# Up projection as seven half-sized products over two pairs of PSUM tiles, with its weight sums made in DRAM

## The chip, the cores and the metric

The kernel runs on one core of one Trainium2 chip. The metric is the device time of one execution in microseconds; lower is better.

## The reference

One layer of a decoder trunk over 512 tokens of width 1024, in float32. Three attention branches (differential, stick-breaking, dilated windows) are read from one input projection, gated and merged, and pass an output projection; then a LayerNorm, and the part that the change touches:

```python
D_MODEL = 1024
SEQ = 512
D_FF = 4 * D_MODEL
PLE_DIM = 256
...
x <- LayerNorm(alpha * x + mixer(x))
x <- LayerNorm(alpha * x + MLP(x) + sigmoid(x W_g) * (p[i] W_p))
```

`MLP(x)` is `square(relu(x @ w_up)) @ w_down`, with `w_up` of 1024 x 4096 and `w_down` of 4096 x 1024.

## The kernel before

Every float32 product is made of three matmuls on rounded operands: each operand is split into a high part (ScalarE casts it, L206 for weights) and a low part (VectorE subtracts, L208), and high x high, high x low and low x high are added in PSUM. Weights come in *chunks* of 128x1024 (512 KB): `fill` issues their loads on SP into a ring of 7 raw tiles, `split_next` turns a raw tile into `wh` and `wl`, which have rings of 7 as well. So a load runs up to 14 chunks ahead of its use.

The work is a list of *items*. Each has a matmul part `mm`, an evacuation `ev` and the chunks that are free after it. The main loop at the end of `trunk` goes through the list with index `n`: it makes sure that the item's chunks are split, emits the previous item's `ev`, splits up to two chunks (`pump`), advances the attention generators by one `step`, emits `mm` and splits again. The tile framework assigns tiles, makes all waits, and places an instruction whose operands are ready ahead of one that still waits, on TensorE too. PSUM has 8 banks: 2 for `mm_bank` and 6 for `at_bank`.

Items 0 to 106 are the input projection and the branches with the attention placed among them; `wout_at` is the index after them. Then come `ple_items`, `wout_items`, `pleg_items` (the gate product, from `x1T`) and `mlp_items`. The first norm runs per 128 tokens in `ln1_gen` during the output projection: VectorE, a power operation on POOL (L440), four transposes per half on TensorE (L515), then the split into `x1hT` and `x1lT` (L518, L519).

The MLP of before: `up(f)` makes 128 hidden columns for all 512 tokens, 8 k x 3 matmuls of 512 columns (L88 to L90, `mm3`), and ScalarE applies Relu and Square. The down projection of the first 7 of 8 blocks is already in seven products instead of eight (a block of 512 hidden columns, 2x2 blocks, sums of operands): `left_first` and `left_rest` make the hidden side's sums, `down` runs a product for 128 tokens (L698 to L700, columns 512). The sums of its weights are made in DRAM by DMAs from POOL: `sum_steps` yields 8 copies and accumulating copies for each block, 56 in all, one for each item from `n` = 30 on; each waits for the latest VectorE split (`st["low"]`). The last block goes through `plain`, with the second norm behind it.

Of the kernel before, what the change touches and what calls it, by code (L numbers as in the profile page):

```python
# [10 lines left out]
F32 = mybir.dt.float32  # L11
# [7 lines left out]
P = 128  # L19
# [37 lines left out]
def trunk(tc, a, out):  # L57
    nc = tc.nc
    es = ExitStack()
    with es:  # L60
# [84 lines left out]
        loads, chunks, placed = [], [], []  # L145
        st = {"dma": 0, "split": 0}
# [47 lines left out]
        def split_next():  # L194
# [9 lines left out]
            for h, lo, a0, a1 in parts:  # L204
                raw = c["from"]["raw"][:, a0:a1]
                i = nc.scalar.copy(h, raw)  # L206
                st["cast"] = getattr(i, "ins", i)
                i = nc.vector.tensor_sub(lo, raw, h.bitcast(F32))  # L208
                st["low"] = getattr(i, "ins", i)
            c["from"]["uses"] -= 1  # L210
# [265 lines left out]
        ln1_done = {}  # L476

# [22 lines left out]
        def ln1_gen(tt):  # L500
# [11 lines left out]
            for h in range(2):  # L512
# [4 lines left out]
                t3 = tp.rearrange("p (k t) -> p k t", k=4)  # L517
                nc.scalar.copy(o, t3)  # L518
                nc.vector.tensor_sub(x1Tl["b"][:, 4 * h:4 * h + 4, q], t3, o.bitcast(F32))  # L519
            ln1_done[tt] = True  # L520
            yield
# [23 lines left out]
        def pleg_items():  # L545
            for half in range(2):
                cs = [chunk(a["wg"][half, c].rearrange("p k n -> p (k n)"), 1024) for c in range(4)]
                for tt in range(4):
# [9 lines left out]
                    def ev(ps, tt=tt, half=half):  # L558
# [6 lines left out]
                        if half and tt > 1:  # L565
                            nc.vector.tensor_sub(acc[tt - 2, 1], acc[tt - 2, 1], t)
# [9 lines left out]
        wsum = [[dram.tile([P, 1024], F32, name=f"wsum{b}_{i}") for i in range(4)] for b in range(7)]  # L576

        def sum_steps():
            def steps(b):
                w = [a["wd"][b, i].rearrange("p k n -> p (k n)") for i in range(4)]  # L580
                t = wsum[b]
                yield t[0], w[0], False
                yield t[2], w[1], False
                yield t[0], w[1], True
                yield t[2], w[3], True
                yield t[1], t[0], False
                yield t[1], w[3], True
                yield t[3], t[1], False
                yield t[3], w[2], True

            def issue(o, i, plus):
# [5 lines left out]
                tc.add_manual_dep(getattr(i, "ins", i), st["low"].name, mybir.DependencyInfo(  # L597
                    mybir.DependencyClass.Sync, mybir.DependencyReason.DATA), reason="spread over the main stream")

            todo = deque(steps(b) for b in range(7))  # L600
# [12 lines left out]
        hraw = {}  # L613
        later = deque()
        left = {}
        keep = {}
        p1s = {}
        v3 = {}
        HB = slice(0, 256)
        HC = slice(256, 512)  # L620

        def mlp_items():
            nb = 7

            def up(f, free=True):
                c = chunk(a["wu"][f].rearrange("p k m -> p (k m)"), 1024)

                def mm(ps):
                    for k in range(8):
                        s = slice(k * P, k * P + P)  # L630
                        mm3(ps, c["h"][:, s], c["l"][:, s], x1T[k], x1Tl[k], k == 0, k == 7)

                def ev(ps):
                    t = slot("hid")
                    nc.scalar.activation(t, ps, AF.Relu)
                    nc.scalar.activation(t, t, AF.Square)
                    left_rest()
                    if f >= 4 * nb:
                        left[f] = split(t)
                        return  # L640
                    hraw[f] = t
                    if f % 2:
                        left_first(f // 2)
                item([c] if free else [], mm, ev)
                return c

            def split(t, cols=slice(0, 512)):
                h = slot("hh", F32R)
                lo = slot("hl", F32R)
                nc.scalar.copy(h[:, cols], t[:, cols])  # L650
                nc.vector.tensor_sub(lo[:, cols], t[:, cols], h[:, cols].bitcast(F32))
                return h, lo

            def left_first(pr):
                e, o = hraw[2 * pr], hraw[2 * pr + 1]
                s12 = slot("s12")
                nc.vector.tensor_sub(s12[:, HB], e[:, HC], o[:, HC])
                nc.vector.tensor_sub(s12[:, HC], e[:, HB], s12[:, HB])
                w = slot("hh", F32R)
                nc.scalar.copy(w[:, HB], e[:, HB])  # L660
                nc.vector.tensor_sub(w[:, HC], e[:, HB], w[:, HB].bitcast(F32))
                left[pr, 1] = (w[:, HB], w[:, HC])
                h, lo = split(s12)
                left[pr, 5] = (h[:, HB], lo[:, HB])
                left[pr, 6] = (h[:, HC], lo[:, HC])
                later.append((pr, s12))

            def left_rest():
                if not later:
                    return  # L670
                pr, s12 = later.popleft()
                e, o = hraw.pop(2 * pr), hraw.pop(2 * pr + 1)
                s34 = slot("s34")
                nc.vector.tensor_sub(s34[:, HB], e[:, HC], e[:, HB])
                nc.vector.tensor_sub(s34[:, HC], o[:, HB], s12[:, HC])
                for t, (p1, p2) in ((s34, (7, 3)), (o, (2, 4))):
                    h, lo = split(t)
                    left[pr, p1] = (h[:, HB], lo[:, HB])
# [824 lines left out]
```

## Time and profile before

| | |
|---|---|
| median of 3 runs | 1081.74 us (1081.31 to 1081.93) |
| profiled execution | 1082.02 us, its span 1080.1 us |
| granted TensorE clock | 0.998 |
| busy | PE 1069.5, PEld 893.5, DVE 661.1, ACT 478.5, POOL 70.0 us |
| up projection in the trace | from 743 to 1039 us, with the down projection among it |
| DMA | 146.18 MB, mean 135 GB/s |

PE is TensorE's matmul, PEld its weight load (beside the matmuls), DVE is VectorE, ACT is ScalarE; a q behind a name is an engine's queue of DMA issues. A line such as "L88 PE MATMUL mm<-x1hT,wh 128*128 128x512 f32 x256 | 99.6, 389 | 0.0" reads: source line, engine, operation, output from inputs, weights and moving shape, count, busy us in all, mean ns of one, idle time before. In an answer in order of time the first two numbers are start and duration in us. A line of the stretches has, after its start and end and its length, for each engine the busy us and the number of instructions (PE, PEld, DVE, ACT, POOL), then the clock, the share of the DMA engines and GB/s.

### The profile page before, as it was taken

The page shows a single profiled execution, that of the slowest core. Times are in us where ns is not written, and L with a number is a line of the kernel's source. Part 1 is how long each engine was busy: PE and PEld are TensorE (multiplying, and loading weights), DVE is VectorE, ACT ScalarE, POOL GpSimd, SP SyncE. Part 2 cuts the span into 40 slices and gives each one's busy share as a digit, 9 for nine tenths or more (in the row PEclk, how much of TensorE's full clock was granted, in tenths as well). Part 3 has the DMA queues.
Part 4 walks back from the last instruction along what each step waited for, and adds up shares of the span by engine and source line. Part 5 has one row for each costly group of instructions (what it writes and reads, how often), then busy time and mean ns, then how long its engine had stood idle before and what let it go on. Part 6 is the DMA issues. An engine that isn't in the chain of part 4 may idle for free.

```text
span 1080.1 us, 13246 instructions
## 1 busy us (share of the span) xinstructions
PE 1069.5 (99%) x4986; PEld 893.5 (83%) x4986; DVE 661.1 (61%) x1223; ACT 478.5 (44%) x795; POOL 70.0 (6%) x111
## 2 busy tenths in 40 slices
PE   9999999999999999999999999999999999999997
PEld 6888788999888888888888888888888888888886
DVE  6888667547254757655443464864575575575676
ACT  6665545425232545464233332233555454454441
POOL 0000200000111011111110020110000000000000
PEclk9999999999999999999999999999999999999999
DMA  8332313153675354567873262242244343444302
GB/s 311 129 117 90 118 40 98 51 183 98 144 208 154 119 127 166 141 162 198 244 193 111 102 231 81 89 166 98 98 158 135 137 156 136 138 146 142 122 1 78
DMA packets 43520, 146.18 MB, mean 135 GB/s; under 512 B 5593, under 2 KB 6505, under 8 KB 43457
## 3 DMA queue, kind: packets, MB, share of 16 engines
q1 hardware_dynamic: 32448, 107.93, 29.4%
q0 software_dynamic: 10432, 36.50, 13.5%
q8 instruction: 39, 0.64, 0.2%
q10 hardware_dynamic: 576, 0.92, 0.2%
q14 instruction: 25, 0.20, 0.1%
HBM read 143.21 MB, written 31.48 MB: 162 GB/s over the span
## 4 chain that ended last, share of the span: by engine, by line
PE 96%; DVE 2%; DMA 1%; ACT 0%; issue 0%; SPq 0%; DVEq 0%
PE mm L88 18%; PE mm L89 18%; PE mm L90 18%; PE mm L317 3%; PE mm L319 3%; PE mm L318 3%; PE mm L698 2%; PE mm L699 2%; PE mm L700 2%; PE at L698 2%; PE at L699 2%; PE at L700 2%; PE mm L556 1%; PE mm L490 1%; PE mm L488 1%; PE mm L554 1%
## 5 line engine op out<-in xcount | busy, mean ns | idle before, releaser
L206 ACT CAST wh<-raw 128x1024 fp32r<-128x1024 f32 (+1 forms) x201 | 207.8, 1035 | 347.1 <-PE mm L89 274.5
L208 DVE TENSOR_TENSOR wl<-raw,wh 128x1024 fp32r<-128x1024 f32 (+1 forms) x201 | 241.0, 1201 | 181.4 <-ACT wh L206 176.9
L88 PE MATMUL mm<-xhT,wh 128*128 128x512 f32 x496 | 196.3, 396 | 0.0
L89 PE MATMUL mm<-xlT,wh 128*128 128x512 f32 x496 | 194.0, 391 | 0.0
L90 PE MATMUL mm<-xhT,wl 128*128 128x512 f32 x496 | 194.0, 391 | 0.0
L90 PEld LDWEIGHTS mm<-xhT,wl 128*128 128x128 f32 x496 | 93.2, 188 | 19.5
L88 PEld LDWEIGHTS mm<-xhT,wh 128*128 128x128 f32 x496 | 93.3, 188 | 18.4 <-issue 0.2
L89 PEld LDWEIGHTS mm<-xlT,wh 128*128 128x128 f32 x496 | 93.2, 188 | 18.2 <-issue 0.2
L88 PE MATMUL mm<-x1hT,wh 128*128 128x512 f32 x256 | 99.6, 389 | 0.0
L89 PE MATMUL mm<-x1lT,wh 128*128 128x512 f32 x256 | 99.6, 389 | 0.0
L90 PE MATMUL mm<-x1hT,wl 128*128 128x512 f32 x256 | 99.6, 389 | 0.0
L317 PE MATMUL mm<-wh,xhT 128*128 128x512 f32 x160 | 64.6, 404 | 0.0
L319 PE MATMUL mm<-wh,xlT 128*128 128x512 f32 x160 | 63.1, 395 | 0.0
L318 PE MATMUL mm<-wl,xhT 128*128 128x512 f32 x160 | 62.9, 393 | 0.0
L90 PEld LDWEIGHTS mm<-x1hT,wl 128*128 128x128 f32 x256 | 48.1, 188 | 10.0
L88 PEld LDWEIGHTS mm<-x1hT,wh 128*128 128x128 f32 x256 | 48.1, 188 | 10.0
L89 PEld LDWEIGHTS mm<-x1lT,wh 128*128 128x128 f32 x256 | 48.1, 188 | 9.9
L319 PEld LDWEIGHTS mm<-wh,xlT 128*128 128x128 f32 x160 | 37.9, 237 | 3.9
L318 PEld LDWEIGHTS mm<-wl,xhT 128*128 128x128 f32 x160 | 38.1, 238 | 3.5
L317 PEld LDWEIGHTS mm<-wh,xhT 128*128 128x128 f32 x160 | 37.9, 237 | 3.5
L698 PE MATMUL mm<-wh,hh 128*128 128x512 f32 x100 | 38.9, 389 | 0.0
L699 PE MATMUL mm<-wl,hh 128*128 128x512 f32 x100 | 38.9, 389 | 0.0
(353 smaller groups left out, 1899.3 us busy)
## 6 DMA issues: line engine op xcount, KB each, us to landing
raw<-in_wt_dram SPq DMA_DIRECT2D x62, 512.0 KB, 3.6
wsum<-in_wd_dram POOLq DMA_DIRECT2D x42, 512.0 KB, 7.3
raw<-in_wu_dram SPq DMA_DIRECT2D x32, 512.0 KB, 3.3
raw<-wsum SPq DMA_DIRECT2D x28, 512.0 KB, 3.3
raw<-in_wd_dram SPq DMA_DIRECT2D x25, 512.0 KB, 3.3
raw<-in_wv_dram SPq DMA_DIRECT2D x20, 512.0 KB, 4.3
wsum<-wsum POOLq DMA_DIRECT2D x14, 512.0 KB, 4.8
raw<-in_wb_dram SPq DMA_DIRECT2D x8, 512.0 KB, 4.1
```

What stands on the lines that cost most here:

```text
L88: nc.tensor.matmul(ps, wh, xh, start=start, stop=False, skip_group_check=True)
L89: nc.tensor.matmul(ps, wh, xl, start=False, stop=False, skip_group_check=True)
L90: nc.tensor.matmul(ps, wl, xh, start=False, stop=stop, skip_group_check=True)
L206: i = nc.scalar.copy(h, raw)
L208: i = nc.vector.tensor_sub(lo, raw, h.bitcast(F32))
L317: nc.tensor.matmul(ps, x1, c["h"][:, s], start=k == 0, stop=False)
L318: nc.tensor.matmul(ps, x1, c["l"][:, s], start=False, stop=False)
L319: nc.tensor.matmul(ps, x2, c["h"][:, s], start=False, stop=k == 7)
L488: nc.tensor.matmul(ps, h[:, q], c["h"][:, s], start=k == 0, stop=False)
L698: nc.tensor.matmul(ps, h[:, q], c["h"][:, s], start=go, stop=False, skip_group_check=True)
L699: nc.tensor.matmul(ps, h[:, q], c["l"][:, s], start=False, stop=False, skip_group_check=True)
L700: nc.tensor.matmul(ps, lo[:, q], c["h"][:, s], start=False, stop=end, skip_group_check=True)
```

## The change

The up projection is made like the down projection: 8 blocks of 512 hidden columns, each as 2x2 blocks (halves of the 1024 inputs, halves of the 512 columns) against 2x2 blocks of `x1` (halves of inputs, halves of tokens), in seven products of a quarter of the work each. Each block is two column tiles (`pair(0)`, `pair(1)`) of four items: `part_a` products 2 and 1 (24 matmuls of 256 columns), `part_b` 7 and 6, `part_c` 5 (12 matmuls), `part_e` 3 and 4; the items of both pairs alternate. A pair uses one `mm_bank` (`x`) and one `at_bank` (`y`) and copies partial results to SBUF in between. A block takes 7 chunks: 3 of `w_up` itself and 4 sums from DRAM.

The sums of `x1` are made from float32 copies that `ln1_gen` now takes of its transposes (`raws`), by `x_forms` during the gate product; `last_form` writes over a quarter of `x1T` when that product is done. The down projection gets its items from `down_parts`, two blocks at a time in five stages that interleave up and down items; `left_step` makes the hidden side's operands one at a time. All products of a block are added to `acc` directly or by a chain that stays in one bank; `plain` takes the leftover products 2 and 4 of two blocks.

The DRAM sums are now 120 (8 x 8 for the up weights, 7 x 8 for the down weights), four blocks at a time, issued 1 or 2 for an item from `n` = 24 to `wout_at` − 15, none until `wout_at` + 4, and then one for every third item; each waits for the fourth last split (`lows`), not the last. The constants of the second norm are loaded at the last stage.

```diff
+                lows.append(st["low"])
             c["from"]["uses"] -= 1
...
                 t3 = tp.rearrange("p (k t) -> p k t", k=4)
+                for kp in range(2):
+                    if tt % 2 == 0:
+                        raws[h, tt // 2, kp] = slot("x1r")
+                    r3 = raws[h, tt // 2, kp].rearrange("p (k t) -> p k t", k=2)
+                    nc.scalar.copy(r3[:, :, tt % 2 * P:tt % 2 * P + P], t3[:, 2 * kp:2 * kp + 2, :])
                 nc.scalar.copy(o, t3)
                 nc.vector.tensor_sub(x1Tl["b"][:, 4 * h:4 * h + 4, q], t3, o.bitcast(F32))
...
-                            nc.vector.tensor_sub(acc[tt - 2, 1], acc[tt - 2, 1], t)
                     item(cs if tt == 3 else [], mm, ev, need=cs)
...
+            def up_steps(m):
+                w = [a["wu"][m, i].rearrange("p k n -> p (k n)") for i in range(4)]
+                a1, a2, a3, a4 = usum[m]
+                yield a1, w[2], False
+                yield a3, w[0], False
+                yield a1, w[3], True
+                yield a3, w[2], True
+                yield a2, a1, False
+                yield a2, w[0], True
+                yield a4, a2, False
+                yield a4, w[1], True
...
+            for m in range(ND):
+                todo.append(up_steps(m))
+                if m < ND - 1:
+                    todo.append(down_steps(m))
             run = []
             while todo or run:
-                while todo and len(run) < 3:
+                while todo and len(run) < 4:
                     run.append(todo.popleft())
...
+        def x_forms():
+            while len(ln1_done) < 4:
+                yield
+            r11, r12, r21, r22 = [[raws[h, th, kp] for kp in range(2)] for h in range(2) for th in range(2)]
+            for kp in range(2):
+                nc.vector.tensor_sub(r11[kp], r11[kp], r12[kp])
+                nc.vector.tensor_sub(r12[kp], r22[kp], r12[kp])
+            yield
+            fs = [split(r12[kp], "t3") for kp in range(2)]
+            forms[7] = [[fs[k // 2][i].rearrange("p (k t) -> p k t", k=2)[:, k % 2, :] for i in range(2)] for k in range(4)]
+            yield
+            for kp in range(2):
+                nc.vector.scalar_tensor_tensor(r22[kp], r22[kp], -1.0, r11[kp], op0=OP.mult, op1=OP.subtract)
+                nc.vector.scalar_tensor_tensor(r21[kp], r22[kp], -1.0, r21[kp], op0=OP.mult, op1=OP.subtract)
+            yield
+            for p, r in ((6, r22), (4, r21)):
+                gs = [split(r[kp], f"t{p}") for kp in range(2)]
+                forms[p] = [[gs[k // 2][i].rearrange("p (k t) -> p k t", k=2)[:, k % 2, :] for i in range(2)]
+                            for k in range(4)]
+                yield
...
+        def last_form():
+            for kp in range(2):
+                r = raws[0, 0, kp].rearrange("p (k t) -> p k t", k=2)
+                h, lo = [x["b"][:, 2 * kp:2 * kp + 2, HC] for x in (x1T, x1Tl)]
+                nc.scalar.copy(h, r)
+                nc.vector.tensor_sub(lo, r, h.bitcast(F32))
+            forms[5] = [(x1T[k][:, HC], x1Tl[k][:, HC]) for k in range(4)]
+            forms[1] = [(x1T[k][:, HB], x1Tl[k][:, HB]) for k in range(4)]
+            forms[2] = [(x1T[k][:, HB], x1Tl[k][:, HB]) for k in range(4, 8)]
+            forms[3] = [(x1T[k][:, HC], x1Tl[k][:, HC]) for k in range(4, 8)]
...
+            wu = a["wu"][m]
+            def operand(n):
+                src = usum[m][n] if isinstance(n, int) else wu[{"11": 0, "12": 1, "21": 2, "22": 3}[n]].rearrange(
+                    "p k n -> p (k n)")
+                cs[n] = chunk(src, 1024)
+            def pair(j):
+                js = slice(256 * j, 256 * j + 256)
+                b = {}
+                def prod(ps, p, n, start, stop):
+                    c = cs[n]
+                    for k in range(4):
+                        s = slice(512 * j + k * P, 512 * j + k * P + P)
+                        mm3(ps, c["h"][:, s], c["l"][:, s], *forms[p][k], start and k == 0, stop and k == 3)
+                def bank(n, new):
+                    def f():
+                        b[n] = new()
+                        return b[n]
+                    return f
+                def add(need, mm, ev, bank):
+                    if j == 0:
+                        for n in need:
+                            operand(n)
+                    item([cs[n] for n in need] if j else [], mm, ev, need=[cs[n] for n in need], bank=bank)
+                def part_a():
+                    def mm(ps):
+                        if 1 not in forms:
+                            last_form()
+                        prod(ps[:, HC], 2, "12", True, True)
+                        b["s"] = slot("up")
+                        nc.scalar.copy(b["s"][:, HB], ps[:, HC])
+                        prod(ps[:, HB], 1, "11", True, False)
+                    def ev(ps):
+                        if j == 0:
+                            hid[m] = [slot("hid") for _ in range(4)]
+                        nc.vector.tensor_add(hid[m][0][:, js], ps[:, HB], b["s"][:, HB])
+                    add(("12", "11"), mm, ev, bank("x", mm_bank))
+                def part_b():
+                    def mm(ps):
+                        prod(ps[:, HB], 7, 2, True, False)
+                        prod(b["x"][:, HB], 6, 1, False, False)
+                    def ev(ps):
+                        nc.scalar.copy(b["s"][:, HC], b["x"][:, HB])
+                        nc.scalar.copy(b["s"][:, HB], ps[:, HB])
+                    add((2, 1), mm, ev, bank("y", at_bank))
+                def part_c():
+                    def mm(ps):
+                        prod(ps[:, HB], 5, 0, False, False)
+                    def ev(ps):
+                        nc.vector.tensor_add(hid[m][3][:, js], ps[:, HB], b["s"][:, HB])
+                    add((0,), mm, ev, lambda: b["x"])
+                def part_e():
+                    def mm(ps):
+                        prod(b["x"][:, HB], 3, 3, False, True)
+                        prod(ps[:, HB], 4, "22", False, True)
+                    def ev(ps):
+                        nc.vector.tensor_add(hid[m][1][:, js], ps[:, HB], b["s"][:, HC])
+                        nc.scalar.activation(hid[m][2][:, js], b["x"][:, HB], AF.Relu)
+                        if j:
+                            for n, sign in ((0, 1.0), (2, 0.0), (1, -1.0), (3, -1.0)):
+                                if sign:
+                                    nc.scalar.activation(hid[m][n], hid[m][n], AF.Relu, scale=sign)
+                                nc.scalar.activation(hid[m][n], hid[m][n], AF.Square)
+                    add((3, "22"), mm, ev, lambda: b["y"])
+                return [part_a, part_b, part_c, part_e]
+            return [x for y in zip(pair(0), pair(1)) for x in y]
...
+        def left_step(m, p):
+            h = hid[m]
+            if m == ND - 1:
+                left[m, p // 2, p % 2] = split(h[p], "h")
+                return
+            if p == 7:
+                h.append(slot("l5"))
+                nc.vector.tensor_sub(h[4], h[3], h[2])
+                nc.vector.tensor_sub(h[2], h[0], h[2])
+            elif p == 6:
+                nc.vector.scalar_tensor_tensor(h[0], h[4], -1.0, h[0], op0=OP.mult, op1=OP.subtract)
+            elif p == 3:
+                nc.vector.scalar_tensor_tensor(h[0], h[1], -1.0, h[0], op0=OP.mult, op1=OP.subtract)
+            left[m, p] = split(h[{1: 0, 7: 2, 6: 0, 4: 3, 5: 4, 2: 1, 3: 0}[p]], "h")
...
+        CHAIN = {1: ("x", True, False, (0, 0), 1), 6: ("x", False, False, (2, 0), 1), 5: ("x", False, False, (2, 1), -1),
+                 3: ("x", False, True, (0, 1), -1), 7: ("y", True, False, (2, 1), -1), 4: ("y", False, True, (2, 0), 1),
+                 2: ("z", True, True, (0, 0), 1)}
+        preps = deque()
...
+        def down_parts(ms, order, kept, both=False):
+            cs = {}
+            out = []
+            for p in order:
+                for r in range(2):
+                    def part(p=p, r=r):
+                        if r == 0:
+                            cs[p] = [down_chunk(m, p) for m in ms]
+                        name, first, last, to, sign = CHAIN[p]
+                        def bank():
+                            if first:
+                                kept[name, r] = at_bank()
+                            return kept[name, r]
+                        def mm(ps):
+                            for n, m in enumerate(ms):
+                                down_mm(ps, m, p, r, cs[p][n], first and n == 0, last and n == len(ms) - 1)
+                        def ev(ps):
+                            t = acc[to[0] + r, to[1]]
+                            if sign > 0:
+                                nc.vector.tensor_add(t, t, ps)
+                            else:
+                                nc.vector.tensor_sub(t, t, ps)
+                            for _ in range(len(ms) if r == 0 or both else 0):
+                                if preps:
+                                    left_step(*preps.popleft())
+                        item(cs[p] if r else [], mm, ev, need=cs[p], bank=bank)
+                    out.append(part)
...
+            order = (1, 7, 6, 4, 5, 2, 3)
+            short = (1, 7, 6, 5, 3)
+            ups = [[0], [1, 2], [3, 4], [5, 6], [7]]
+            downs = [[], [0], [1, 2], [3, 4], [5, 6], []]
+            kept = {}
+            for stage in range(5):
+                us = [x for m in ups[stage] for x in up_parts(m)]
+                ds = down_parts(downs[stage], short if stage == 4 else order, kept, stage == 4) if downs[stage] else []
+                if stage == 4:
+                    ln2_at[0] = len(items)
+                done, lead = 0, 3
+                for n, u in enumerate(us):
+                    u()
+                    if n == len(us) - 1:
+                        nxt = downs[stage + 1]
+                        todo = [(m, p) for p in (short + (2, 4) if stage == 3 else order) for m in nxt]
+                        if stage == 4:
+                            todo = [(ND - 1, i) for i in range(4)]
+                        items[-1]["then"] = (todo, len(nxt))
+                    while done < len(ds) and (n == len(us) - 1 or done * (len(us) - lead) < (n - lead + 1) * len(ds)):
+                        ds[done]()
+                        done += 1
+            wd = a["wd"][ND - 1]
+            c2 = [down_chunk(m, 2) for m in (5, 6)]
+            cs = {(i % 2, i // 2): chunk(wd[2 * (i % 2) + i // 2].rearrange("p k n -> p (k n)"), 1024)
+                  for i in range(4)}
+            c4 = [down_chunk(m, 4) for m in (5, 6)]
+            plain(cs, c2, c4, kept)
...
             if prev is not None:
                 prev[0]["ev"](prev[1])
+                todo, lead = prev[0].get("then", ((), 0))
+                preps.extend(todo)
+                for _ in range(lead):
+                    left_step(*preps.popleft())
...
-            if n >= 30:
+            for _ in range((1 + (n % 4 == 0)) if 24 <= n < wout_at - 14 else (n % 3 == 0) if n > wout_at + 4 else 0):
                 next(sum_steps_, None)
...
-            if n == wout_at + 24:
+            if n == ln2_at[0]:
                 ln_consts("ln2_g", "ln2_b")
...
-        "wu": col_tiles(w_up[0]),
+        "wu": c(w_up[0].reshape(2, 4, 128, 8, 2, 2, 128).transpose(3, 5, 0, 2, 4, 1, 6).reshape(8, 4, 128, 2, 512)),
```

More of the change, by code (lines that the diff above doesn't have):

```diff
@@ new lines, in trunk, with split @@
+        raws = {}
+        forms = {}
+        hid = {}
+        left = {}
+        def split(t, name):
+            h, lo = slot(name + "h", F32R), slot(name + "l", F32R)
+            nc.scalar.copy(h, t)
+            nc.vector.tensor_sub(lo, t, h.bitcast(F32))
+            return h, lo
+        def x_forms():
[18 more added lines that the diff above has]
+                yield
```

324 lines of the change are left out of this document (105 added, 219 removed).

## The prediction

> **What bounds the kernel now.** I read the busy shares first, then the chain that ended last, then the waits of TensorE, then the groups of instructions by shape, and last the order of time where the change sits.
>
> ```profile
> span 1080.1 us, 13246 instructions
> ...
> PE 1069.5 (99%) x4986; PEld 893.5 (83%) x4986; DVE 661.1 (61%) x1223; ACT 478.5 (44%) x795; POOL 70.0 (6%) x111
> ...
> PE 96%; DVE 2%; DMA 1%; ACT 0%; issue 0%; SPq 0%; DVEq 0%
> ...
> PE at L298 <- ACT wh L206: 1.3, 1, 1.3
> PE at L857 <- DVE zero L854: 1.3, 1, 1.3
> PE at L1143 <- DVE lg L1138: 0.2, 1, 0.2
> ```
>
> TensorE is busy 99% of the span, the chain is 96% matmul, and between the start and the tail TensorE waits once, for 0.2 us. Time can be won only by giving it less to do, and every wait put into its stream costs in full. The 0.39 us of a "busy" matmul holds its drain; the price of one in a stream is the distance between starts:
>
> ```profile
> 799.96 0.39 PE L90 MATMUL mm<-x1hT,wl 128*128 128x512 f32 x1
> 800.19 0.39 PE L698 MATMUL mm<-wh,hh 128*128 128x512 f32 x1
> 802.91 0.39 PE L698 MATMUL at<-wh,hh 128*128 128x512 f32 x1
> ...
> 1069.24 0.39 PE L753 MATMUL at<-wh,hl 128*128 128x512 f32 x1
> 1069.47 0.28 PE L751 MATMUL at<-wh,hh 128*128 128x256 f32 x1
> 1069.67 0.69 DVE L772 TENSOR_TENSOR xn<-xn,at 128x512 f32<-128x512 f32 x1 [0.47 <-PE at L753]
> 1071.38 0.28 PE L752 MATMUL at<-wl,hh 128*128 128x256 f32 x1
> ```
>
> From 800.19 to 802.91 lie 12 starts of 512 columns: 0.2267 us each. From 1069.47 to 1071.38 lie 16 starts of 256 columns: 0.1194 us each, each with a weight load of its own. Half the columns cost 52.7% of the time, not 50%.
>
> **Term 1, the up projection: −13.6 us.** Before, 32 column tiles x 8 k x 3 matmuls are 768 of 512 columns (L88, L89, L90 on `x1hT`, 256 each): 768 x 0.2267 = 174.1 us.
>
> ```profile
> L88 PE MATMUL mm<-x1hT,wh 128*128 128x512 f32 x256 | 99.6, 389 | 0.0
> L89 PE MATMUL mm<-x1lT,wh 128*128 128x512 f32 x256 | 99.6, 389 | 0.0
> L90 PE MATMUL mm<-x1hT,wl 128*128 128x512 f32 x256 | 99.6, 389 | 0.0
> ```
>
> After, 8 blocks x 7 products x 2 column tiles x 4 k x 3 are 1344 of 256 columns: 160.5 us. A seventh product less in eight is worth 21.8 us; the shorter matmul takes 8.2 of them back. At 0.1295 us per start nothing would be left. The down projection keeps its count (7 blocks x 7 products x 12, and a plain last block), as do the tail and all before the first norm.
>
> The Trainium skill ("TensorE: Matmul & The Clock Gate", section "Back-to-back issue gap") gives N/2.4 + 2.5 ns, that is 215.8 and 109.2 ns; by it, an estimate, the term would be 165.8 − 146.7 = 19.1 us. The trace doesn't agree (226.7 and 119.4 ns), and the rows decide.
>
> **Term 2, a copy between two products in one bank: +3.2 us (0 to 9.9).** `part_a` puts product 2 into columns 256 to 511 of a PSUM bank, copies it out on ScalarE, and then puts product 1 into columns 0 to 255 of the same bank. The tile framework orders the users of a bank as a whole. The attention shows that shape: L1157 writes 128 columns of one bank for a query block, L1161 reads them, the next L1157 writes the neighbouring columns, and no reading overlaps the next writing.
>
> ```profile
> 392.77 0.60 PE L1157 MATMUL at<-da_v,wT 128*128 128x128 f32 x4
> 393.41 0.28 ACT L1161 ACTIVATE scr<-at 128x128 f32<-128x128 f32 x1 [5.33 <-PE at L1157]
> 399.15 0.83 PE L1157 MATMUL at<-da_v,wT 128*128 128x128 f32 x6
> ...
> L329 ACT CAST sb_v<-mm 128x256 fp32r<-128x256 f32 x8 | 2.9, 368 | 8.4 <-PE mm L319 4.6 <-DVE sb_v L330 3.8
> ...
> 386.00 0.75 DVE L1138 SCALAR_TENSOR_TENSOR lg<-lg,rr,lg 128x512 f32<-128x512 f32 x1
> 386.81 0.44 PE L1143 MATMUL at<-ident,lg 128*128 128x128 f32 x2 [0.20 <-DVE lg L1138]
> ```
>
> Such a wait at its shortest: 0.28 us for the last matmul to drain, 0.04 to the reader (1069.24 + 0.39 to 1069.67), 0.37 for the copy (L329), 0.06 back to TensorE (386.75 to 386.81), less the 0.12 that the next start would have taken: 0.63 us. There are 16 (8 blocks x 2), so 9.9 us where TensorE stands idle, nothing where another matmul whose operands are ready is placed into the gap. Before, the attention's matmuls are placed that way among the projection's, and the one wait left is 0.2 us. That is the nearest row, so I take 16 x 0.2 = 3.2.
>
> **Term 3, work on VectorE and ScalarE: +2.5 us (0 to 7.6).**
>
> ```profile
> 765.00:1040.00 275.00, 275.00 (x1214) 227.76 (x1214) 171.16 (x238) 136.16 (x187) 0.00 (x0) 1.00 0.38 130
> ...
> L208 DVE TENSOR_TENSOR wl<-raw,wh 128x1024 fp32r<-128x1024 f32 x193 | 235.5, 1222 | 172.9 <-ACT wh L206 168.4 <-PE at L1157 2.8
> L705 DVE TENSOR_TENSOR xn<-xn,mm 128x512 f32<-128x512 f32 x50 | 34.1, 681 | 7.0 <-PE mm L700 7.0
> L651 DVE TENSOR_TENSOR hl<-s,hh 128x512 fp32r<-128x512 f32 x28 | 19.2, 687 | 4.3 <-ACT hh L650 4.2
> L657 DVE TENSOR_TENSOR s<-hid,hid 128x256 f32<-128x256 f32 x14 | 5.9, 425 | 0.0
> L206 ACT CAST wh<-raw 128x1024 fp32r<-128x1024 f32 x193 | 202.8, 1052 | 327.9 <-PE mm L89 255.4 <-PE mm L700 20.4 <-PE mm L490 19.2
> L636 ACT ACTIVATE hid<-hid 128x512 f32<-128x512 f32 x32 | 20.3, 634 | 1.0
> L635 ACT ACTIVATE hid<-mm 128x512 f32<-128x512 f32 x32 | 18.9, 591 | 0.0
> L650 ACT CAST hh<-s 128x512 fp32r<-128x512 f32 x28 | 17.4, 620 | 11.4 <-DVE s L658 8.5 <-DVE s L675 2.9
> ```
>
> In the 275 us of both MLP products VectorE works 171 us (62%) and ScalarE 136 (50%). The change adds 24 weight chunks (56 for 32), 29.3 us by L208 and 25.2 by L206, and 48 additions of 128x256 out of PSUM, 20.4 us by L657. ScalarE loses 32 x 1.225 us (L635, L636) and gets 64 pieces of 0.37 and 56 activations of 0.634: +20. The operands' sums and splits shrink by some 5 us on VectorE (14 pairs at 5 x 0.42 and 46 lows at 0.687 become 28 sums of some 0.70 and 53 lows). So VectorE would be busy 216 of 261 us (83%), ScalarE 181 (69%): no bound on the mean, but little room. The tightest place: in a stage with two blocks, product 7 of the down projection waits for operands made after product 1's first half. VectorE has 0.68 + 6 x 0.69 + 0.68 + one chunk of 1.22 = 6.7 us to do while TensorE has 12 x 0.2267 + 12 x 0.1194 = 4.15 us ahead of it: 2.5 us short, three times, if nothing else is placed there. I take one of the three. The last stage (17 chunks, 6 additions, 12 + 4 lows, 8 sums, 10 additions of 0.68) comes to 46.8 us of VectorE against 47.3 of TensorE.
>
> **Terms at nothing.** The ScalarE copies added in `ln1_gen` (4 x 0.37 = 1.5 us) and the new forms hide behind the gate product: the last piece of `x1hT` is there at 708.45, the product that needs it starts at 698.4 + 3 x 5.44 (24 x 0.2267) = 714.7.
>
> ```profile
> 707.19 1.26 ACT L518 CAST x1hT<-at 128x512 fp32r<-128x512 f32 x2 [2.43 <-PE at L515]
> ...
> L554 PE MATMUL mm<-wh,x1hT x64: 389/389/475, 698.4 to 742.4; 128*128 128x512 f32 x64
> ...
> 450.00:640.00 190.00, 190.00 (x868) 157.87 (x867) 93.57 (x148) 73.69 (x118) 24.08 (x36) 1.00 0.61 166
> ...
> q1 hardware_dynamic: 32448, 107.93, 29.4%
> q0 software_dynamic: 10432, 36.50, 13.5%
> ...
> wsum<-in_wd_dram POOLq DMA_DIRECT2D x42, 512.0 KB, 7.3
> ...
> wsum<-wsum POOLq DMA_DIRECT2D x14, 512.0 KB, 4.8
> ```
>
> That leaves 4.7 us; without it the copies would cost their 1.5 us once. DRAM sums rise from 56 (42 + 14) to 120. A sum takes 2.1 us of all DMA engines (29.4 of q0's 36.5 MB in its 13.5% of the span, by 56), a 512 KB load 1.5 (q1 by 206). In the MLP the share rises from 0.38 by 24 loads (0.14) and some 30 sums (0.24) to 0.76; before the norm 87 sums for 56 add about 0.1 to the 0.61. Loads run up to 14 chunks ahead, so a load twice as late costs nothing; if that cover is gone, each late one costs up to 7.3 us. `lows` makes a sum wait for the fourth last split, not the last: POOL, where the norm's power operation queues behind sums, waits less.
>
> **Sum.** The profiled execution took 1082.02 us (span 1080.1), 0.3 above the median of 1081.74. 1082.0 − 13.6 + 3.2 + 2.5 = 1074.1; I give 1074.
>
> **Rivals.** *The bank's copy comes late (slower).* ScalarE is in order. After a block's last part it has a split of 1.05 us, 0.37 + 7 x 0.634 = 4.8 us of Relu and Square, and two more splits: 8.0 us. The next block's copy is due 2.72 + 1.43 = 4.15 us after that part, so it ends at 8.4 and TensorE stands 4.3 us, at seven of the eight block starts; the other nine copies cost 0.63: 35.8 us together, 1082.0 − 13.6 + 35.8 + 2.5 = 1106.7. With half of the wait filled by later products it is about 1089. It decides from 13.6 us of such waits on. For it: the shape above and ScalarE's longer queue; against it: before, TensorE never waits for a bank. The Trainium skill ("PSUM — Partial Sum Buffer", section "PSUM bank collisions raise a hardware error") states that two engines may not be in one bank at a time, disjoint columns included; by that rule the copy can't run beside product 1, and the trace agrees as far as L1157 and L1161 show.
>
> *VectorE sets the pace.* At 83%, each of the 48 additions finds a split of 1.22 us ahead of it: 1.22 + 0.43 + 0.1 against the 1.43 of one product leaves 0.32 x 48 = 15 us: 1083.4 to 1086. Against it: most additions have two or more products before their bank is needed.
>
> *Sums or loads come late*: five loads at 7.3 us, 1105. Against it: the shares above.
>
> **How the numbers follow.** Under 0.2% (2.2 us) a measurement can't tell a change here. The forecast's case, 1068 to 1079.5: 0.57. Terms 2 and 3 near their upper ends, or VectorE's pace, landing within 2.2 us of before: 0.08. Slower 0.35: the late copy 0.25, VectorE 0.05, sums 0.05. The range goes from 1067 to 1097, which takes in the half-filled late copy and leaves out about 0.2.
>
> **What would show it.** Matmuls of 256 columns at a distance of 0.119 us between 743 and 1035; VectorE near 83% there. Waits of TensorE named by the copy in `part_a` above 13.6 us, or a chain with several per cent of ScalarE or VectorE, would make the forecast wrong; waits for `raw` or `usum`, the last rival.

## The result and the profile after

The changed kernel takes 1073.12 us (median of 4 runs, 1072.90 to 1073.38) where the kernel before takes 1081.84 on the same chip (4 runs, 1081.31 to 1083.27): a ratio of 0.9917, 95% interval 0.9900 to 0.9935. The forecast was 1074.0, range 1067 to 1097. The profiled execution took 1072.9 us, its span 1071.2; before they were 1082.02 and 1080.1.

The page of the profile after, the same parts as shown of before, and below them TensorE's waits (us in total, times, longest):

```profile
span 1071.2 us, 14785 instructions
...
PE 1060.4 (99%) x5562; PEld 910.4 (85%) x5562; DVE 705.6 (66%) x1262; ACT 517.5 (48%) x890; POOL 113.4 (11%) x175
...
PE 96%; DVE 2%; ACT 0%; DMA 0%; issue 0%; SPq 0%; DVEq 0%
```

```profile
PE at L965 <- DVE zero L962: 1.3, 1, 1.3
PE at L300 <- ACT wh L207: 0.4, 1, 0.4
PE at L1251 <- DVE lg L1246: 0.2, 1, 0.2
```

The shape is that of before: TensorE 99% busy, a chain 96% matmul, the same three kinds of wait and no new one. 576 matmuls more are done in less time. Two more parts of the page of after, the groups of instructions and the DMA queues, and then its windows (VectorE's busy time is the third pair of numbers, ScalarE's the fourth; the last three are granted clock, DMA share and GB/s):

```profile
L88 PE MATMUL mm<-x1hT,wh 128*128 128x256 f32 x256 | 73.8, 288 | 0.0
...
L88 PEld LDWEIGHTS mm<-x1hT,wh 128*128 128x128 f32 x256 | 48.8, 191 | 4.7 <-ACT up L729 2.9
...
q1 hardware_dynamic: 35904, 120.51, 32.4%
q0 software_dynamic: 19648, 70.06, 25.4%
```

```profile
450.00:640.00 190.00, 190.00 (x868) 157.87 (x867) 93.65 (x146) 73.67 (x117) 32.31 (x48) 1.00 0.70 198
765.00:1030.00 265.00, 265.00 (x1702) 240.45 (x1702) 207.27 (x267) 164.48 (x252) 17.80 (x27) 1.00 0.73 230
```

In the MLP VectorE is 78% busy and ScalarE 62% (before 62 and 50), and the DMA engines 0.73 (before 0.38). The copy in `part_a` (L729 here) shows only as 2.9 us of waits of the weight load.

The 8.9 us of the span can be placed. From 742 us on I took the distance from each matmul's start to the next and subtracted the price of its shape (0.1194 us for 256 columns, 0.2267 for 512). What is left over adds up to 4.6 us after and to nothing before: 13.6 − 4.6 = 9.0 saved in the MLP. The end of the program, from the last matmul's start, takes 9.03 us where it took 7.88. And the MLP starts 1.0 us earlier (742.05 for 743.07). That is no more than kernels with the same code up to there differ (741.72 to 742.91), so the change need not have won it. 9.0 − 1.15 + 1.0 = 8.85. The experiments say what the 4.6 and the 1.15 are.

### The profile page after: what moved, and what is told of

Read it like the earlier page. It is cut to its first block, busy times and chain, and to the rows that moved or that the text cites. A ratio compares the mean times of both kernels' runs of the same rounds, so it can differ in the third digit from the quotient of the medians.

```text
span 1071.2 us, 14785 instructions
## 1 busy us (share of the span) xinstructions
PE 1060.4 (99%) x5562; PEld 910.4 (85%) x5562; DVE 705.6 (66%) x1262; ACT 517.5 (48%) x890; POOL 113.4 (11%) x175
## 4 chain that ended last, share of the span: by engine, by line
PE 96%; DVE 2%; ACT 0%; DMA 0%; issue 0%; SPq 0%; DVEq 0%
PE mm L88 16%; PE mm L89 16%; PE mm L90 16%; PE at L795 4%; PE at L796 4%; PE at L797 4%; PE mm L319 3%; PE mm L321 3%; PE mm L320 3%; PE at L90 1%; PE at L88 1%; PE at L89 1%; PE mm L566 1%; PE mm L493 1%; PE mm L491 1%; PE mm L565 1%
## 5 line engine op out<-in xcount | busy, mean ns | idle before, releaser
L207 ACT CAST wh<-raw 128x1024 fp32r<-128x1024 f32 (+1 forms) x225 | 232.2, 1034 | 310.1 <-PE mm L89 238.8
L209 DVE TENSOR_TENSOR wl<-raw,wh 128x1024 fp32r<-128x1024 f32 (+1 forms) x225 | 269.7, 1203 | 118.9 <-ACT wh L207 114.9
L88 PE MATMUL mm<-x1hT,wh 128*128 128x256 f32 x256 | 73.8, 288 | 0.0
L795 PE MATMUL at<-wh,hh 128*128 128x512 f32 x188 | 73.7, 392 | 0.0
L796 PE MATMUL at<-wl,hh 128*128 128x512 f32 x188 | 73.7, 392 | 0.0
L797 PE MATMUL at<-wh,hl 128*128 128x512 f32 x188 | 73.1, 389 | 0.0
L89 PE MATMUL mm<-x1lT,wh 128*128 128x256 f32 x256 | 72.3, 283 | 0.0
L90 PE MATMUL mm<-x1hT,wl 128*128 128x256 f32 x256 | 71.8, 283 | 0.0
L621 POOL DMA_DIRECT2D usum<-in_wu_dram x32 | 30.5, 962 | 157.5 <-DVE wl L209 152.7
L797 PEld LDWEIGHTS at<-wh,hl 128*128 128x128 f32 x188 | 35.3, 188 | 7.7
```

Of the source, the lines that this page charges most:

```text
L88: nc.tensor.matmul(ps, wh, xh, start=start, stop=False, skip_group_check=True)
L89: nc.tensor.matmul(ps, wh, xl, start=False, stop=False, skip_group_check=True)
L90: nc.tensor.matmul(ps, wl, xh, start=False, stop=stop, skip_group_check=True)
L621: i = nc.gpsimd.dma_start(o, i, accum_op=OP.add, max_dma_last_dim=4096)
L795: nc.tensor.matmul(ps, h[:, q], c["h"][:, s], start=go, stop=False, skip_group_check=True)
L796: nc.tensor.matmul(ps, h[:, q], c["l"][:, s], start=False, stop=False, skip_group_check=True)
```

## The experiments

The theory is that TensorE alone sets the time: seven products of 256 columns save 13.6 us, and a few us are lost around the copy that stands between two products of one bank. The rivals are that the loss is not the copy's but that of VectorE's load or of the DRAM sums, or that the copy is harmless whatever the order of TensorE. Each run has its ratio to before, with its interval; all times are medians.

**Half the columns, no product saved.** In the kernel before:

```diff
-mm3(ps, c["h"][:, s], c["l"][:, s], x1T[k], x1Tl[k], k == 0, k == 7)
+for q in (HB, HC):
+    mm3(ps[:, q], c["h"][:, s], c["l"][:, s], x1T[k][:, q], x1Tl[k][:, q],
+        k == 0 and q is HB, k == 7)
```

> The kernel before, with each of the up projection's 768 matmuls of 512 columns made as two of 256 (the same products, no seventh left out). If 256 columns cost 0.1194 us by start, as in the tail of before, 1536 x 0.1194 = 183.4 us stand for 174.1: 9.3 us slower than before, about 1091. By the page's N/2.4 + 2.5 it would be 1.9 us slower, about 1084. If the shorter matmul costs nothing extra in a long stream, 1082, and the change's gain would have to be 21.8 us with 13 lost elsewhere.

Measured: 1091.99 us, ratio 1.0094 (1.0079 to 1.0109), 10.2 over before: the theory's price, and not a free split. The Trainium skill ("TensorE: Matmul & The Clock Gate", section "Back-to-back issue gap") gives 109.2 ns for 256 columns by its formula; the trace doesn't agree, with 119.8 here. The order of time of this run, around a visit to the down projection's 512 columns (a *visit* is a stretch of 512-column matmuls between 256-column ones):

```profile
813.50 0.28 PE L90 MATMUL mm<-x1hT,wl 128*128 128x256 f32 x1
813.62 0.40 PE L700 MATMUL mm<-wh,hh 128*128 128x512 f32 x1
...
817.51 0.39 PE L702 MATMUL mm<-wh,hl 128*128 128x512 f32 x1
817.73 0.28 PE L88 MATMUL mm<-x1hT,wh 128*128 128x256 f32 x1
```

From 813.62 to 817.73 are 18 starts: 4.11 us, where 18 x 0.2267 are 4.08. Visits of 24 take as much too long: 0.027 us is the mean of the 25 visits of 18 or 24. The change of width costs, not each matmul.

**The copy moved out of the pair.** In the kernel after the copy waits until both products stand in the bank:

```diff
 prod(ps[:, HC], 2, "12", True, True)
 b["s"] = slot("up")
-nc.scalar.copy(b["s"][:, HB], ps[:, HC])
 prod(ps[:, HB], 1, "11", True, False)
 def ev(ps):
     ...
+    nc.scalar.copy(b["s"][:, HB], ps[:, HC])
```

> The kernel after, with the copy of product 2 moved from between the two products of part_a to the item's evacuation. If the copy is what opens the gaps of about 0.2 us before product 1 (some 13 of 16, 2.6 us together), they close: about 1070.5. Rival: copy and addition now stand together after product 1 and hold up product 6 in the same bank, which comes one product or more later: 1073 or above, with the gap before the t6 matmuls instead.

Measured: 1070.63 us, ratio 0.9896 (0.9881 to 0.9911), 2.5 below the kernel after. What the start distances leave over falls from 4.6 to 1.8: 2.8 us for 16 copies, 0.17 each. The weight load's group on the page of this run has no copy among its releasers any more:

```profile
L88 PEld LDWEIGHTS mm<-x1hT,wh 128*128 128x128 f32 x256 | 49.0, 191 | 1.6
```

**TensorE held to the order of the items.** The kernel after, with each MLP item's matmuls behind the last of the item before (`st["mm"]`, which the lines left out set behind each product):

```diff
...
+with ExitStack() as line:
+    if n > wout_at + 24 and n < len(items) - 9:
+        line.enter_context(tc.issue_after(st["mm"]))
     for _ in it["mm"](ps) or ():
```

> The kernel after, with TensorE held to the order of the items in the MLP: a matmul of a later item no longer goes ahead of one that waits. If products of later items placed into the copy's wait are what kept it small, the late copy costs what the rival of the prediction says, 7 x 4.3 + 9 x 0.63 = 35.8 us for the 2.6 of now: about 1106, with TensorE waiting for the copy. If ScalarE has the copy ready early anyway, only 16 x 0.63 = 10: about 1080. If order doesn't matter, 1073.

Measured: 1089.96 us, ratio 1.0075 (1.0060 to 1.0090): 16.8 over the kernel after, and slower than before. TensorE's waits, and the order of time at two of the sixteen copies:

```profile
PE mm L88 <- ACT up L730: 15.4, 16, 1.3
```

```profile
766.81 0.62 ACT L768 ACTIVATE hid<-hid 128x512 f32<-128x512 f32 x1
767.35 0.35 ACT L730 COPY up<-mm 128x256 f32<-128x256 f32 x1
767.60 0.63 ACT L769 ACTIVATE hid<-hid 128x512 f32<-128x512 f32 x1
...
877.22 0.28 PE L90 MATMUL mm<-x1hT,wl 128*128 128x256 f32 x1
877.42 1.04 ACT L208 CAST wh<-raw 128x1024 fp32r<-128x1024 f32 x1 [4.80 <-PE mm L89]
878.37 0.36 ACT L730 COPY up<-mm 128x256 f32<-128x256 f32 x1
878.79 0.39 PE L88 MATMUL mm<-x1hT,wh 128*128 128x256 f32 x1 [1.29 <-ACT up L730]
```

Product 2 ends, a cast of 1.04 us stands ahead of the copy, and product 1 starts 1.57 us after the last start instead of 0.12. ScalarE had no work piled up: before that cast it stood idle for 4.80 us. At a block's start only one piece of the block before stands ahead of the copy (767.35 lies between two of them). Eight gaps are of 1.57 us, eight of 0.74 to 1.18. The same kind of place in the kernel after, in its first block:

```profile
746.49 0.28 PE L90 MATMUL mm<-x1hT,wl 128*128 128x256 f32 x1
746.61 0.28 PE L88 MATMUL at<-t3h,wh 128*128 128x256 f32 x1
746.69 1.05 ACT L207 CAST wh<-raw 128x1024 fp32r<-128x1024 f32 x1 [2.63 <-PE mm L89]
...
747.64 0.37 ACT L729 COPY up<-mm 128x256 f32<-128x256 f32 x1
747.69 0.28 PE L88 MATMUL at<-t3h,wh 128*128 128x256 f32 x1
747.81 0.28 PE L89 MATMUL at<-t3l,wh 128*128 128x256 f32 x1
748.06 0.39 PE L88 MATMUL mm<-x1hT,wh 128*128 128x256 f32 x1
748.28 0.28 PE L89 MATMUL mm<-x1lT,wh 128*128 128x256 f32 x1
```

Such a cast stands before the copy here too, but matmuls of the up projection's product 7 (`t3`) fill the time up to 747.81. Product 1 starts 0.05 us after the copy has ended, and two distances of 0.25 and 0.22 us where 0.12 is usual are all that is lost.

**One product of TensorE left out.** In the kernel after `prod(ps[:, HB], 5, 0, False, False)` becomes `pass`.

> The kernel after without the matmuls of product 5 of the up projection (192 of 256 columns); its loads, splits, copies and additions stay. If TensorE alone sets the time in the MLP, 192 x 0.1196 = 23.0 us less: 1050. If VectorE sets the pace, as one rival has it, less than half of that: 1062 or more.

Measured: 1049.86 us, ratio 0.9707 (0.9692 to 0.9721), 23.3 below the kernel after; 192 x 0.1196 are 23.0. TensorE's time comes off in full, so nothing else was within 23 us of setting the pace.

**VectorE lighter and heavier.** One kernel adds 8 columns of each accumulator instead of all, one adds a pass over it:

```diff
-if sign > 0:
-    nc.vector.tensor_add(t, t, ps)
-else:
-    nc.vector.tensor_sub(t, t, ps)
+nc.vector.tensor_add(t[:, 0:8], t[:, 0:8], ps[:, 0:8])
```

```diff
     nc.vector.tensor_sub(t, t, ps)
+nc.vector.tensor_scalar(t, t, 0.0, None, op0=OP.add)
```

> The kernel after with the 66 additions of down products to acc cut from 512 columns to 8, so that some 40 us of VectorE's work is left out and its waits stay. If VectorE has room, 1073 (within 1 us). If its queue holds up TensorE somewhere (the forecast gave it 2.5 us, the rival 15), 2.5 us less or more.

> The kernel after with one pass of VectorE over 128x512 added behind each of the 66 additions of down products: some 66 x 0.45 = 30 us more, from 78% of the MLP's time to about 90%. If there is room, 1073 to 1076. If VectorE is near setting the pace, 1085 or more. It tells where the margin ends, not what the change cost.

Measured: 1073.05 us, ratio 0.9921 (0.9906 to 0.9936), and 1072.96, ratio 0.9928 (0.9911 to 0.9944). The windows of the three kernels, light, after, heavy:

```profile
765.00:1020.00 255.00, 255.00 (x1646) 231.84 (x1647) 174.82 (x256) 155.32 (x239) 17.81 (x27) 1.00 0.75 239
```

```profile
765.00:1020.00 255.00, 255.00 (x1646) 231.71 (x1646) 198.82 (x256) 155.34 (x239) 17.80 (x27) 1.00 0.76 239
```

```profile
765.00:1020.00 255.00, 255.00 (x1646) 231.87 (x1646) 214.07 (x305) 155.18 (x239) 17.80 (x27) 1.00 0.75 239
```

VectorE at 69, 78 and 84% leaves the same time within 0.2 us, and TensorE does its 1646 instructions in each. I had expected the heavy one at 90%; the 49 passes in the window take 0.3 us each, less than I gave them. How it would go beyond 84% was not tried.

**No sums in DRAM.** The kernel after, with the 120 sums not issued and the loads reading the raw blocks (the lines of the loads are left out here):

```diff
-issue(*s)
...
```

> The kernel after without the 120 DRAM sums; the loads that read a sum read a block of the weights instead, so as many bytes come in, and the result is not the reference's. If the sums are off the path, 1073; if their traffic is what widens the 512-column matmuls of the down projection from 0.2267 to 0.229 us by start, 588 x 0.002 = 1.2 us less, about 1072. Rival, sums or loads that come late: 3 us or more less.

Measured: 1071.96 us, ratio 0.9907 (0.9891 to 0.9924), 1.16 below the kernel after. What the start distances leave over in the MLP stays (4.5 for 4.6), so the sums and their traffic cost TensorE nothing there. The gain is at the end. There each engine has DRAIN instructions, and GpSimd's longest is the one that counts here. The lines give its durations (nanoseconds: shortest, median, longest) before (56 sums), after (120) and in this run (none):

```profile
L1499 POOLq DRAIN  x3: 46/102/5189, 1074.1 to 1079.8; - x3
```

```profile
L1613 POOLq DRAIN  x3: 46/102/6334, 1064.1 to 1070.9; - x3
```

```profile
L1613 POOLq DRAIN  x3: 46/102/3804, 1064.4 to 1069.9; - x3
```

From 5.19 to 6.33 us is the 1.15 by which the end grew from before to after. Without sums the drain is 2.53 us shorter than after, but the end only 1.33: the drain is then no longer what ends last.

**The old pacing.** The kernel after with one sum an item from item 30 on, as in the kernel before: another pace, and no pause around the first norm:

```diff
-for _ in range((1 + (n % 4 == 0)) if 24 <= n < wout_at - 14 else (n % 3 == 0) if n > wout_at + 4 else 0):
+for _ in range(1 if n >= 30 else 0):
```

> The kernel after with the pace of before for the DRAM sums: one for each item from n = 30 on, without a pause, so that the last 40 fall into the output projection, the norm and the gate product. If the pause hides nothing (POOL's power operation waits for one DMA issue of 1 us, and the gate product has 4.7 us to spare), 1073. If the pause is needed, TensorE waits at the transposes or the first gate products: 1074 to 1080.

Measured: 1080.58 us (10 runs, 1077.92 to 1081.79), ratio 0.9989 (0.9979 to 0.9998): the new pacing, pace and pause together, is worth 7.5 us, most of the gain. The loss was not where I expected it, but before the norm, ahead of the output projection's matmuls (`oTh`). TensorE's wait, the order of time around the load of `pTraw` (512 KB, issued by GpSimd), and two windows of this run:

```profile
PE mm L88 <- DVE graw L387: 4.9, 1, 4.9
```

```profile
621.68 0.81 POOL L621 DMA_DIRECT2D usum<-in_wu_dram  x1 [9.44 <-DVE wl L209]
622.21 1.12 POOL L621 DMA_DIRECT2D dsum<-in_wd_dram  x1
624.78 0.59 POOL L1108 DMA_DIRECT2D pTraw<-in_pT_dram  x1 [1.46 <-PE mm L90]
634.83 1.04 ACT L1109 CAST pThl<-pTraw 128x1024 fp32r<-128x1024 f32 x1 [8.72 <-DMA pTraw<-in_pT_dram]
635.90 1.22 DVE L1110 TENSOR_TENSOR pThl<-pTraw,pThl 128x1024 fp32r<-128x1024 f32 x1 [7.75 <-ACT pThl L1109]
637.05 0.68 DVE L387 TENSOR_TENSOR graw<-graw,mm 128x512 f32<-128x512 f32 x1
637.78 0.80 PE L88 MATMUL mm<-oTh,wh 128*128 128x512 f32 x1 [4.92 <-DVE graw L387]
...
641.79 0.46 PE L88 MATMUL mm<-oTh,wh 128*128 128x512 f32 x1
```

```profile
615.00:635.00 20.00, 17.87 (x79) 14.45 (x77) 4.78 (x5) 4.15 (x7) 3.08 (x4) 1.00 0.99 245
637.70:641.80 4.10, 4.02 (x10) 3.19 (x11) 4.03 (x6) 0.68 (x2) 1.92 (x4) 0.50 0.25 80
```

With the DMA engines at 0.99 (0.39 in the same window of the kernel after), the load issued at 624.78 lands 10.0 us later (3.9 in the kernel after). Two engines wait for it, and what stands behind in their order waits too: ScalarE's cast holds up the next weight cast, VectorE's split holds up the evacuation at L387, and TensorE, which needs L387's bank, stands for 4.9 us. Then it runs at a granted clock of 0.50: nine starts from 637.78 to 641.79 take 4.01 us for 2.04. 4.9 + 2.0 = 6.9 of the 7.5. The Trainium skill ("TensorE: Matmul & The Clock Gate", section "What's actually happening") says that the array falls to half its clock after an idle window of about 3.4 us and comes back after as long a busy one. The trace agrees on the half, with 0.50 after 4.92 us of standing, and roughly on the way back, with 4.1 us from the first start at 637.78 to the full clock. It shows the fall sooner: the mean granted clock from 633.00 to 637.70 is 0.72, so it was halved from about 635.1 on, only 2.2 us after the last matmul's end (632.48 + 0.39).

**A pause of four items.** The old pacing, with no sums at the four items up to the load of `pTraw`:

```diff
-for _ in range(1 if n >= 30 else 0):
+for _ in range(1 if n >= 30 and not wout_at - 12 <= n <= wout_at - 9 else 0):
```

> The kernel after with the sums at the old pace (one an item from item 30 on), and a pause of four items alone, up to and with the item that issues the load of pT. In the run of the old pace without any pause, this load landed 10.0 us after its issue instead of 3.9, ScalarE's cast waited 8.7 us for it, and TensorE stood 4.9 us behind that and then started some ten matmuls every 0.43 us; that run was 7.5 us slower than the kernel after. Theory: the pause's worth is this one load, behind four or five sums under way. Then the wait of 4.9 us is gone and the time is 1073 to 1075. Rival: with sums at one an item around the norm the DMA engines are full (0.99 of the window 640 to 695) and another load is late: a wait of TensorE for some other cast or for the norm's pieces, 1076 to 1080.

Measured: 1074.86 us, ratio 0.9934 (0.9920 to 0.9948). The load lands in 4.4 us and the wait of 4.9 is gone: 5.7 of the 7.5 us hang on this one load. A window of this run, GpSimd at the next place at which a sum comes in the way, and TensorE's wait there:

```profile
615.00:635.00 20.00, 20.00 (x90) 16.57 (x89) 9.37 (x12) 6.81 (x8) 3.50 (x6) 1.00 0.77 257
```

```profile
679.50 0.81 POOL L621 DMA_DIRECT2D dsum<-in_wd_dram  x1 [1.59 <-DMA dsum<-dsum]
683.66 0.54 POOL L623 DMA_DIRECT2D usum<-usum  x1 [3.35 <-DMA usum<-in_wu_dram]
684.21 0.59 POOL L442 TENSOR_TENSOR lr<-lr,mhalf 128x1 f32<-128x1 f32 x1
```

```profile
PE at L518 <- DVE xn L446: 1.3, 1, 1.3
```

GpSimd waits at 683.66 for an earlier sum before it comes to the norm's power operation; VectorE waits 2.7 us for that, and TensorE's transposes 1.3. This is the kind of wait that the rival of late sums names, in a small size.

**The plain copies issued by SyncE.** Of the 120 sums, 60 are copies without addition; in the late copy's kernel and in the kernel after they go from GpSimd to SyncE (SP), which issues the weight loads:

```diff
-i = nc.gpsimd.dma_start(o, i, max_dma_last_dim=4096)
+i = nc.sync.dma_start(o, i, max_dma_last_dim=4096)
```

> The late copy (1070.6) with the sums' plain copies, 60 of the 120, issued by SyncE instead of GpSimd. The drain at the end on GpSimd was 3.80 us with no sums, 5.19 with 56 and 6.33 with 120. Theory: it grows with the number of DMAs that GpSimd issued, so that 60 fewer take it to about 5.2 and the time to 1069.5. Rival: the copies stand in SyncE's order between the weight loads and hold these up, or the drain does not depend on which engine issued them: 1070.6 or more, with waits for casts in the MLP or before the norm.

> The kernel after with the sums' 60 plain copies issued by SyncE, and the copy of product 2 where it was. By the theory that the drain grows with the DMAs that GpSimd issued: 1072.0, with the drain at about 5.2 us instead of 6.33 and nothing else moved. By the rival that they hold up SyncE's weight loads: over 1073.

Measured: 1070.11 us, ratio 0.9893 (0.9878 to 0.9907), and 1072.90, ratio 0.9919 (0.9905 to 0.9933). The first is the lowest time of the kernels that leave nothing out, 0.5 below the late copy, but the intervals of the two overlap almost wholly. The second lies only 0.2 below the kernel after, and my theory of the drain fell. The drain of the late copy's kernel with SyncE:

```profile
L1613 POOLq DRAIN  x3: 46/93/6052, 1061.5 to 1068.1; - x3
```

It is 0.28 us shorter, not 1.1, so it doesn't go with the number of DMAs that GpSimd issued. That it goes with the accumulating ones (none 3.80, 28 in the kernel before 5.19, 60 here 6.05) would fit, and is not shown. TensorE got no new wait; VectorE waits once for the load of a sum, 1.7 us in the late copy's kernel.

## Why the prediction was right

It came out within 0.9 us, by the mechanism it named: TensorE sets the time, and fewer but shorter matmuls save 13.6 us less what the copies cost. Not each term was of its size, and the closeness of the sum is partly luck.

**Term 1, −13.6: right.** The distances in an undisturbed stretch of 256 columns are 0.1196 us for the 0.1194 taken from the tail (1344 of them: 0.3 us). Splitting alone cost 10.2 where 9.3 was expected, and leaving out one product gave 23.3 for 23.0.

**Term 2, +3.2: right in kind and near in size.** 2.8 us by the start distances, 2.5 by the time, against 16 x 0.2. That other matmuls fill the gap is what makes it small: held to the items' order, the same copies cost 15.4 us of waits. The size is luck: the row it was taken from is a wait of TensorE for VectorE's `lg`, not for a bank. The upper end was slightly off in its sum as well: 16 x 0.63 are 10.1, not 9.9.

**Term 3, +2.5: wrong, it is nothing.** TensorE has no wait for the operands of the down projection's product 7 in the trace, and taking 24 us from VectorE or adding 15 changes nothing. The step that failed is that product 7 "waits for operands made after product 1's first half". The first of the three places, in the kernel after (L781 and L782 make product 7's sums, L655 its low parts; product 1 starts at 834.99, product 7 at 841.89):

```profile
834.22 0.69 DVE L782 TENSOR_TENSOR hid<-hid,hid 128x512 f32<-128x512 f32 x1
834.99 0.40 PE L795 MATMUL at<-wh,hh 128*128 128x512 f32 x1
...
837.29 0.68 DVE L655 TENSOR_TENSOR hl<-hid,hh 128x512 fp32r<-128x512 f32 x1
...
841.89 0.40 PE L795 MATMUL at<-wh,hh 128*128 128x512 f32 x1
```

The last of product 7's sums is done at 834.91, before product 1 begins, and its last low part at 837.97, 3.9 us before product 7 starts: VectorE's work had been moved forward. TensorE had just those matmuls ahead that the forecast gave it, 12 of 512 columns and 12 of 256, and needed no more. The other two places look the same, with 3.9 us to spare in the second and 2.7 or more in the third. VectorE was 78% busy, not 83.

**Two terms were missing.** 512-column matmuls were taken at 0.2267 throughout. A visit to them among 256-column ones takes 0.027 us longer than that, be it 6, 12 or 24 matmuls long: 1.3 us for the 48 visits in the kernel after. (Three of its visits end in a copy's gap and take some 0.065 more; in the late copy's kernel none does.) And GpSimd's drain adds 1.15 at the end; the sum had no term for the end of the program. These two, 2.45 us, stand about where term 3's 2.5 stood, and the 1.0 us by which the MLP started earlier makes up most of the rest: the sum was right by 0.9 us partly because errors balanced.

**Terms at nothing: right in the stages they named.** The DMA share in the MLP is 0.73 to 0.76 for the 0.76 given, before the norm 0.70 for 0.7, and the sums cost TensorE nothing there. The gate product takes 44.7 us in both kernels, from its first start to the MLP's, so the copies in `ln1_gen` are hidden.

**The rivals.** The late copy is real, but its price was too high at the step "a split, 4.8 us of Relu and Square, and two more splits: 8.0 us". ScalarE's instructions are not laid down block after block: those whose operands came earlier stand earlier, and the copy finds one cast or one piece ahead of it. So even with TensorE in order the gaps were 0.74 to 1.57 us and not 4.3, and the time 1090, not 1106.7. That this is near the 1089 of the half-filled case is chance: there, later products fill half of long waits, while here none could and the waits themselves were short. VectorE's pace fell with the light and the heavy run. Late sums are the rival that the change itself had answered: with the old pacing it comes to 1080.6, mostly by one load of 512 KB, and a pause of four items avoids most of it. I had given the new pacing no term at all; its worth, 7.5 us, is nearly as large as the whole result.

## What to carry to other kernels

Where one engine is busy 99%, count its instructions at the distance between starts of the very shape, and add a small toll for each change of width; other engines' load is not a price until it delays an operand. Before charging a wait for operands, look when they are really made: an instruction whose inputs are ready may be placed well ahead of where the code has it. A copy between two uses of one bank is cheap as long as other ready matmuls can be placed there, so look for what can fill the gap, or put the copy behind both uses. Background DMA hurts at the one load that is issued only just before someone needs it: pause it around that load, and count the program's end too.

## What the runs showed that was not expected

- A visit of TensorE to 512-column matmuls from 256-column ones costs 0.027 us, whether it is 6, 12, 18 or 24 matmuls long (seen in three kernels).
- GpSimd's last drain takes 3.80 us with no DRAM sums, 5.19 with 56, 6.33 with 120, and 6.05 when 60 of the 120 are issued elsewhere.
- A load landing in 10.0 us instead of 3.9 cost TensorE 4.9 us of standing and 2.0 us at half clock after it; the clock had fallen 2.2 us after the last matmul's end.
